# A decoder layer on one core: gate mask written first and rows added onto it by DMA, pooling means on ScalarE, two loads later, 187 pieces in another order

## The chip, the core and the metric

The program runs on one core of a Trainium2 chip. The core has a matrix engine (TensorE; its matmuls are "PE" in the profile and its weight loads "PEld"), three engines for elementwise work (VectorE "DVE", ScalarE "ACT", GpSimd "POOL"), and SyncE ("SP"), which here only issues transfers. Each engine takes its instructions strictly in the order of its own queue and waits on semaphores where it needs another engine's or a transfer's result. Transfers from SP's queue and from POOL's queue share 16 DMA engines.

The metric is the device time of one execution in microseconds, the median over runs. Lower is better.

## What is computed

One layer for 256 tokens of width 1024 in float32. The input `x` is normalised, multiplied with a wide matrix `w_in`, and the columns of the product feed three mixers side by side: a pooling mixer, a gated recurrent mixer with four heads (mLSTM) and causal attention with eight heads. Their outputs go through `w_out` and are added to `x`; then comes a gated feed-forward part with a short convolution.

```python
def pool_mixer(xp, w_pool, scale):          # four groups of 64 channels, windows 2, 4, 8, 16
    ...
        win_sum = cs[:, 1:, g] - cs[:, lo, g]
        outs.append(win_sum / cnt[None, :, None] - xg[:, :, g])   # cnt is smaller than w in the first tokens
    ...
def mlstm_chunkwise(q, k, v, i_pre, f_pre):
    ...
        logd = jnp.where(causal, g[..., :, None] - g[..., None, :] + ic[..., None, :], -jnp.inf)
        ...
        w = jnp.einsum('bhtd,bhsd->bhts', qc, kc) * jnp.exp(logd - mt[..., None])
...
        x = x + mix @ w_out[l]
        h2 = rmsnorm(x, ln2_g[l])
        u = causal_dwconv(h2 @ w_up[l], ffn_conv[l])
        x = x + (jax.nn.silu(u[..., :D_FF]) * u[..., D_FF:]) @ w_down[l]
```

## The kernel before

**Products.** To keep float32 accuracy on TensorE, each operand is split into a rounded part `hi` (ScalarE, line 214, rounded to the fp32r type) and the rest `lo` (VectorE, line 221, `raw - hi`). A product is then three matmuls: hi·hi, hi·lo and lo·hi. The weights come in "units" of 1 MB, loaded by SP into four rotating buffers `raw`, and each unit is split in two halves: pieces `("hi", u, q)` and `("lo", u, q)`. Units 0 to 10 are slices of `w_in`: 0 `of`, 1 `vi`, 2 `mq`, 3 `mk`, 4 and 5 the first attention heads (A), 6 `pool`, 7 and 8 the other heads (B), 9 and 10 the attention values (V). Then follow four units of `w_out`, eleven of `w_up` and eleven of `w_down`.

**The first microseconds.** `x` arrives transposed in eight slabs of 128 rows each together with the `of` columns (line 254), every slab a transfer of its own. VectorE scales each slab by the norm's gain (`first_full`, piece `("f", p)`, line 390, into `h_f`); TensorE multiplies it in plain float32 with the `of` weights (pieces `("of", t, p)`, line 511; the slab of `h_f` is the stationary operand, so its weight load waits for the `f` piece). The slabs are also squared in four quarters on ScalarE (`("sq", q)`, line 410; added up on VectorE, line 414), and split into `h_hi` (`("h", q)`, ScalarE, line 394) and `h_lo` (`("l", q)`, VectorE, line 398). The gain `g1` lies in the buffer of the first four slabs, so that buffer is free for unit 3 only when the last `f` piece has run.

**Order.** The mixer part of the program is a set of closures ("pieces"). Each has a place, a number from the table `PLACE` (line 44) or a default, and the pieces are emitted in the order of these numbers; an assertion keeps every piece behind those that it needs. The matmul groups stand at whole numbers from 4 on (`("b", n)`), so the table says between which matmul groups, and in which order on every engine, the small work is done. Nothing is rearranged later: a queue's order is the order of the places.

**Small work that the change touches.** The gates of the mLSTM go through a chain of scans on VectorE (pieces `pg`, `ga`, `gm`, `gs`, lines 640 to 660); the running maxima `mr` of the four heads are written to DRAM (`bm`, line 666), read back broadcast to all 128 partitions into `mb` (`br`, line 669), and GpSimd overwrites in the two diagonal blocks of each head what lies above the diagonal with 1e30 (`bs`, `affine_select`, line 674), so that `exp(a - mb)` gives zero there (`("wt", h)`, line 691). `("ct", name, j)` are the three taps of the short convolution on VectorE (line 539), `sig` the sigmoids on ScalarE between two table loads (lines 272, 548, 551), `("si", key)` the products that make the SiLU (line 555), `("mS", j)` the mLSTM's scores on TensorE (line 702), `("me", h)` their product with the decay (line 707), `("mN", t)` the product with the values (line 714). For attention, `("hq", ...)` and `("hs", ...)` are squares and their sums per head (lines 578, 584), `("kn", g)` the factors of the keys (lines 570 to 605), `("ke", g, t)` the scaled keys (line 610), `("kT", g)` and `("qT", g)` their transposes on TensorE (line 619), `("S", g, j)` the scores, `("PT", ...)` the transposed probabilities (line 816), `("pt", ...)` their copies (lines 822, 824) and `("O", g, j)` the products with the values (line 835).

**Pooling.** `pool_z` (lines 841 to 858) forms, for each half of the 256 channels, the window sums on GpSimd by doubling the width, copies the group with the smaller window along, multiplies with the table of 1/count (`rcnt`, 2 x 256 columns of `con`) and subtracts the channel itself, all in one piece. `pool_t` (line 862) multiplies the result with `pool_w`.

**Loads.** SP issues, in order: the eight slabs, unit 1 in two parts, unit 2, the parameters `par`, the constants `con` (512 KB, line 263), unit 3, the rows of `x` (`xs`, two transfers of 512 KB, line 403; first used by the residual after `w_out`), units 4 and so on. GpSimd's own queue carries, behind the pooling, the transfers `far` (line 1220) that prepare sums of `w_down` weights for the last stage.

Of the kernel before, what the change touches and what calls it, by code (L numbers as in the profile page):

```python
# [117 lines left out]
U_UP = U_OUT + N_OUT  # L118
U_DOWN = U_UP + NPAIR
N_UNITS = U_DOWN + N_DOWN  # L120


C_RCNT = 0
C_MN = C_RCNT + 2 * S
C_PW = C_MN + 256
C_END = C_PW + 2 * P


Q_G2 = 0
# [1392 lines left out]
```

## Time and profile before

| | |
|---|---|
| median of 3 runs | 295.83 us (295.75 to 296.02) |
| the profiled execution's own time | 295.97 us |
| its span, first to last instruction | 294.2 us |
| PE busy | 289.5 us, 98% |
| DVE / ACT / POOL busy | 260.1 / 209.3 / 44.7 us |
| TensorE clock granted | 1.00 throughout |

The span is 1.8 us shorter than the execution's time. In the views, a row of the timeline has a start, a duration, the engine, the line, the operation, `out<-in`, the shapes and how many instructions it stands for; in brackets is the engine's idle time ahead of it and what ended that. Instructions of one engine overlap in their pipelines: the time from one start to the next, not the duration, is what an instruction costs in its queue. A plain float32 matmul is two passes and shows as two.

### The profile page before, as it was taken

Reading aid. Unit: us, or ns where it says so; the run is one execution under the profiler, and the core shown is the slowest. Engines: PE = TensorE matmul, PEld = TensorE weight load, DVE = VectorE, ACT = ScalarE, POOL = GpSimd, SP = SyncE. Lnnn points to the kernel's source line nnn. Section 1 sums busy time; section 2 is a strip of 40 time slices with the busy share of each in tenths; the row PEclk is TensorE's granted clock in tenths of the full one; section 3 lists DMA queues with packets and bytes.
Section 4 is the critical chain, followed back from the end, with each engine's and each line's share of the span. In section 5 each row is a group of like instructions: output and inputs, shape, how many; then the busy total and the mean of one; then the engine's idle time right before and its main releaser. Section 6 shows DMA issues by size and latency. Waiting matters only on the chain.

```text
span 294.2 us, 4565 instructions
## 1 busy us (share of the span) xinstructions
PE 289.5 (98%) x1606; PEld 245.6 (83%) x1606; DVE 260.1 (88%) x518; ACT 209.3 (71%) x395; POOL 44.7 (15%) x73
## 2 busy tenths in 40 slices
PE   8999999999999999999999999999999999999995
PEld 4899888788778778888888888888988988888884
DVE  1978998999977757769999999999999989999992
ACT  3777779679895736987787787687677478786700
POOL 1000104724100005105015105105102110000000
PEclk9999999999999999999999999999999999999999
DMA  7999974079876576999998999997988988998003
GB/s 225 406 419 373 331 276 167 2 177 320 189 280 238 192 286 241 192 320 341 282 353 203 317 337 211 348 303 195 333 270 185 280 226 273 331 342 341 3 1 143
DMA packets 16599, 75.39 MB, mean 256 GB/s; under 512 B 1844, under 2 KB 2240, under 8 KB 10688
## 3 DMA queue, kind: packets, MB, share of 16 engines
q1 hardware_dynamic: 10384, 60.29, 54.3%
q0 software_dynamic: 6048, 14.68, 25.0%
q8 instruction: 12, 0.20, 0.3%
q10 hardware_dynamic: 144, 0.13, 0.1%
q14 instruction: 11, 0.09, 0.1%
HBM read 74.04 MB, written 15.73 MB: 305 GB/s over the span
## 4 chain that ended last, share of the span: by engine, by line
PE 87%; DVE 6%; ACT 3%; issue 2%; DMA 1%
PE up L1170 25%; PE up L1173 13%; PE wo L885 8%; PE dn L885 6%; PE m L1294 6%; PE dn L1294 5%; PE of L511 3%; DVE lo L221 2%; PE V L497 1%; PE V L499 1%; PE V L498 1%; PE upr L1103 1%; PE upr L1102 1%; PE upr L1101 1%; PE B L497 1%
## 5 line engine op out<-in xcount | busy, mean ns | idle before, releaser
L221 DVE TENSOR_TENSOR lo<-raw,hi 128x1024 fp32r<-128x1024 f32 (+2 forms) x74 | 83.7, 1148 | 4.6 <-ACT hi L214 4.6
L1170 PE MATMUL up<-h,hi 128*128 128x512 f32 x320 | 76.3, 391 | 0.0
L214 ACT ACTIVATE hi<-raw 128x1024 fp32r<-128x1024 f32 (+2 forms) x74 | 70.9, 983 | 6.2 <-DMA raw<-in_w 4.0
L1170 PEld LDWEIGHTS up<-h,hi 128*128 128x128 f32 x320 | 58.9, 188 | 11.4
L1173 PEld LDWEIGHTS up<-h,lo 128*128 128x128 f32 x320 | 41.0, 191 | 1.5
L1173 PE MATMUL up<-h,lo 128*128 128x256 f32 x320 | 41.6, 283 | 0.0
L1191 DVE SCALAR_TENSOR_TENSOR fy<-z,par,fy 128x255 f32<-128x255 f32 (+1 forms) x80 | 33.3, 479 | 0.0
L1220 POOL DMA_DIRECT2D far<-far x14 | 11.8, 840 | 106.6 <-DMA far<-in_w 55.4
L1220 POOL DMA_DIRECT2D far<-in_w x28 | 22.7, 1246 | 7.2 <-DMA far<-in_w 7.2
L1187 ACT ACTIVATE fy<-z,par 128x256 f32<-128x256 f32 x40 | 18.1, 502 | 1.7 <-DVE z L1180 1.2
L1201 ACT ACTIVATE fy<-fy 128x256 f32<-128x256 f32 x20 | 8.4, 418 | 12.2 <-DVE fy L1191 12.2
L1180 DVE TENSOR_TENSOR z<-up,zl 128x512 f32<-128x512 f32 x20 | 13.8, 688 | 3.0 <-ACT zl L1178 2.9
L1178 ACT ACTIVATE zl<-up 128x512 f32<-128x512 f32 x20 | 11.9, 594 | 4.0 <-PE up L1173 4.0
L221 DVE TENSOR_TENSOR lo<-more_raw,hi 128x1024 fp32r<-128x1024 f32 x12 | 14.6, 1218 | 0.0
L1294 PE MATMUL m<-ph,h 128*128 128x512 f32 x42 | 14.1, 389 | 0.0
L214 ACT ACTIVATE hi<-more_raw 128x1024 fp32r<-128x1024 f32 x12 | 12.6, 1053 | 0.0
L1208 ACT ACTIVATE a_hi<-a_sv 128x256 fp32r<-128x256 f32 (+1 forms) x16 | 5.7, 369 | 8.4 <-DVE a_sv L1203 8.4
L885 PE MATMUL wo<-hi,mix_hi 128*128 128x512 f32 x32 | 11.2, 411 | 0.0
L1329 ACT ACTIVATE ph<-sum 128x1024 fp32r<-128x1024 f32 x8 | 8.4, 1055 | 3.1 <-PE dn L1294 2.3
L885 PE MATMUL wo<-lo,mix_hi 128*128 128x512 f32 x32 | 10.6, 392 | 0.0
L885 PE MATMUL wo<-hi,mix_lo 128*128 128x512 f32 x32 | 10.6, 392 | 0.0
L1330 DVE TENSOR_TENSOR pl<-sum,ph 128x1024 fp32r<-128x1024 f32 x8 | 9.7, 1217 | 0.0
(331 smaller groups left out, 642.7 us busy)
## 6 DMA issues: line engine op xcount, KB each, us to landing
raw<-in_w SPq DMA_DIRECT2D x33, 1024.0 KB, 8.8
far<-in_w POOLq DMA_DIRECT2D x14, 512.0 KB, 11.1
more_raw<-in_w SPq DMA_DIRECT2D x6, 1024.0 KB, 8.6
sum<-far SPq DMA_DIRECT2D x4, 1024.0 KB, 6.8
far<-in_w POOLq DMA_DIRECT2D x14, 256.0 KB, 12.7
far<-far POOLq DMA_DIRECT2D x14, 256.0 KB, 7.4
more_raw<-far SPq DMA_DIRECT2D x3, 1024.0 KB, 8.2
raw<-in_w SPq DMA_DIRECT2D x4, 768.0 KB, 5.5
```

Of the source, the lines that this page charges most:

```text
L214: nc.scalar.activation(hi_t[u][:, s], raw_t[u][:, s], AF.Copy)
L221: nc.vector.tensor_sub(lo_t[u][:, s], raw_t[u][:, s], hi_t[u][:, s].bitcast(F32))
L885: nc.tensor.matmul(acc[t, c][:, :n], a, b[:, k, o:o + n], start=st and i == 0, stop=sp and i == 2)
L1170: nc.tensor.matmul(up_t[i][:, j], a, h_2[:, k].rearrange("p c t -> p (c t)"), start=k == 0, stop=False)
L1173: nc.tensor.matmul(up_t[i][:, j, :S], a, h_hi[:, k, :], start=False, stop=k == KT - 1)
L1178: nc.scalar.activation(zl, ps[:, :, S:], AF.Copy)
L1180: nc.vector.tensor_add(z, ps[:, :, :S], zl)
L1187: nc.scalar.activation(y_t[i, j], up_t[i][j], AF.Copy, scale=pcol(Q_FC + i + NPAIR * j + 4 * NPAIR))
L1191: nc.vector.scalar_tensor_tensor(y[:, d:], up_t[i][j][:, :S - d], pcol(Q_FC + i + NPAIR * j + 2 * NPAIR * tap), y[:, d:], op0=ALU.mult, op ...
L1220: nc.gpsimd.dma_start(s_far[i][:, at, :], src[:, block:block + 1, :].to_broadcast([P, at.stop - at.start, 512]), **({"accum_op": ALU.add} ...
L1294: nc.tensor.matmul(dst, a[x], b[y], start=start and n == 0, stop=stop and n == 2)
L1330: nc.vector.tensor_sub(l[:, s], src, h[:, s].bitcast(F32))
```

## The change

1. **Mask first.** GpSimd writes the mask into `mb` at the start of the program (1e30 above the diagonal, 0 elsewhere, from a constant). `spread_back` then adds the two diagonal blocks of the maxima onto it with an accumulating transfer from GpSimd's queue (512 KB), and SP loads only the third block (256 KB). The piece `bs` is gone; `br` now needs `setup`, and the decays wait for `br`.
2. **Pooling.** The window sums use two tiles in turn per half; the copies of the smaller group are gone. The first 16 tokens of each group are corrected by a small product on GpSimd (64 x 16), and the means are four ScalarE operations (64 x 256, a new piece `("pla", j)`) that multiply by 1/window. GpSimd subtracts the channel behind them. The 1/count table shrinks from 512 to 32 columns, so that `con` is 273 KB.
3. **Loads.** `con` is issued behind unit 6 and `xs` behind unit 11.
4. **Order.** 187 entries of `PLACE` differ. Two rows of the table, before and now:

```diff
-    ("f", 0): 1.75, ("of", 0, 0): 1.754813, ("f", 1): 1.7552, ("f", 2): 1.758, ("f", 3): 1.760807, ("of", 1, 0):
+    ("f", 0): 1.750626, ("of", 0, 0): 1.750984, ("sq", 0): 1.75217, ("f", 1): 1.753604, ("f", 3): 1.760807,
...
+    def load_rest(u):
+        if u == 6:
+            nc.sync.dma_start(con, consts)
+        if u == 11:
+            for t in range(NT):
+                nc.sync.dma_start(xs[:, t], x[t * P:(t + 1) * P])
...
+    mb = mpool.tile([P, 3, 4, P], F32, name="mb")
     nc.gpsimd.memset(ones, 1.0)
+    later_keys = mb.rearrange("p b h c -> p (b h) c")[:, :8, :]
+    nc.gpsimd.affine_select(later_keys, nc.const_aps.tensor_like(0.0, later_keys), [[0, 8], [1, P]], ALU.is_ge, -NEG,
+                            base=0, channel_multiplier=-1)
...
     def spread_back():
-        nc.sync.dma_start(mb, sb["far"].partition_broadcast(P))
-
-    def mask_max():
-
-        d = mb.rearrange("p b h c -> p (b h) c")[:, :8, :]
-        nc.gpsimd.affine_select(d, d, [[0, 8], [1, P]], ALU.is_ge, -NEG, base=0, channel_multiplier=-1)
+        nc.gpsimd.dma_start(mb[:, :2], sb["far"][:2].partition_broadcast(P), accum_op=ALU.add)
+        nc.sync.dma_start(mb[:, 2:], sb["far"][2:].partition_broadcast(P))
...
     def pool_z(j):
-        z = mid(f"plz{j}", 16 + S)
-        nc.gpsimd.memset(z[:, :16], 0.0)
+        z, *two = [mpool.tile([P, 16 + S], F32, name=f"pl{n}{j}") for n in "zab"]
+        for tile_ in (z, *two):
+            nc.gpsimd.memset(tile_[:, :16], 0.0)
         nc.vector.tensor_mul(z[:, 16:], ps_t["pool", j], rb)
...
-        d = mid(f"pld{j}")
-        nc.gpsimd.tensor_mul(d, cur[:, 16:], rcnt[:, j, :])
-        nc.gpsimd.tensor_sub(d, d, z[:, 16:])
+        sums, width = [z], 1
+        for n in range(2 + 2 * j):
+            r = slice(64 * (n == 1 + 2 * j), P)
+            cur = sums[-1]
+            sums.append(two[n % 2])
+            nc.gpsimd.tensor_add(two[n % 2][r, 16:], cur[r, 16:], cur[r, 16 - width:16 + S - width])
+            width *= 2
+        sb["plz", j], sb["pls", j] = z, sums[-2:]
+        for h in range(2):
+            r = slice(64 * h, 64 * h + 64)
+            few = sums[h - 2][r, 16:32]
+            nc.gpsimd.tensor_mul(few, few, con[r, C_RCNT + 16 * j:C_RCNT + 16 * j + 16])
+
+    def pool_mean(j):
+        d = sb["pls", j][1][:, 16:]
+        for h in range(2):
+            r = slice(64 * h, 64 * h + 64)
+            nc.scalar.activation(d[r, :], sb["pls", j][h][r, 16:], AF.Copy, scale=con[r, C_INV + j:C_INV + j + 1])
+        nc.gpsimd.tensor_sub(d, d, sb["plz", j][:, 16:])
         sb["pld", j] = d
```

**Place 1: ACT and DVE while the slabs arrive.** `sq` are the squares and their sums, `h<-h_f` the quarters of `h_hi` (ACT) and `h_lo` (DVE), `h_f<-head` the scaled slabs, `hi<-raw` the split of unit 1. ACT before:

```order
L410 ACTIVATE sq_112<-head_84 128x512
L394 ACTIVATE h_101<-h_f 128x2x256 x2
L410 ACTIVATE sq_112<-head_85 128x512
L410 ACTIVATE sq_112<-head_84 128x512
L394 ACTIVATE h_101<-h_f 128x2x256
L410 ACTIVATE sq_112<-head_85 128x512
```

and now, behind it the same stretch of DVE, before and now:

```order
L422 ACTIVATE sq_115<-head_88 128x512 x2
L408 ACTIVATE h_104<-h_f 128x2x256 x2
L422 ACTIVATE sq_115<-head_89 128x512 x2
L408 ACTIVATE h_104<-h_f 128x2x256
L226 ACTIVATE hi_163<-raw_90 128x520 x3
```

```order
L390 TENSOR_SCALAR h_f<-head_85,head_84 128x256
L398 TENSOR_TENSOR h_101<-h_f,h_101 128x2x256 x2
L390 TENSOR_SCALAR h_f<-head_85,head_84 128x256 x2
L414 TENSOR_TENSOR sq_112<-sq_112 128x512
L398 TENSOR_TENSOR h_101<-h_f,h_101 128x2x256
L390 TENSOR_SCALAR h_f<-head_85,head_84 128x256
```

```order
L404 TENSOR_SCALAR h_f<-head_89,head_88 128x256
L412 TENSOR_TENSOR h_104<-h_f,h_104 128x2x256
L404 TENSOR_SCALAR h_f<-head_89,head_88 128x256 x2
L426 TENSOR_TENSOR sq_115<-sq_115 128x512
L412 TENSOR_TENSOR h_104<-h_f,h_104 128x2x256 x2
L404 TENSOR_SCALAR h_f<-head_89,head_88 128x256
```

On ACT the second square (slabs 2 and 3) stands ahead of the first two quarters of `h_hi`, and the fourth ahead of the third quarter. On DVE the `h_lo` operation that is first in its row is now that of the second quarter, which needs ACT's second quarter; the first quarter's stands, with the third's, ahead of the last slab.

**Place 2: DVE around the SiLU products**, from the last taps on (`mqT`, `mkT` with their head pair's number, `sg` the sigmoids, `gm` the output gate, `lo6`, `lo7` splits of units 6 and 7, `plz0` the first pooling half, `akAss` sums of the keys' squares). Before:

```order
L555 TENSOR_TENSOR mkT0_489<-mkT0_489,sg_510 128x256
L555 TENSOR_TENSOR mqT0_432<-mqT0_432,sg_508 128x256
L555 TENSOR_TENSOR mkT1_491<-mkT1_491,sg_514 128x256
L555 TENSOR_TENSOR mqT1_436<-mqT1_436,sg_512 128x256
L221 TENSOR_TENSOR lo7_519<-raw7_352,hi7_475 128x1024
L558 TENSOR_TENSOR gm_122<-gm_122,con_81 128x256 x2
```

and now:

```order
L566 TENSOR_TENSOR mqT0_436<-mqT0_436,sg_508 128x256
L569 TENSOR_TENSOR gm_124<-gm_124,con_81 128x256
L566 TENSOR_TENSOR mkT1_491<-mkT1_491,sg_514 128x256
L233 TENSOR_TENSOR lo6_463<-raw6_265,hi6_395 128x1024
L595 TENSOR_REDUCE akAss_531<-akAsq0_524 128x4
L233 TENSOR_TENSOR lo7_533<-raw7_354,hi7_478 128x1024
L566 TENSOR_TENSOR mkT0_488<-mkT0_488,sg_510 128x256
L233 TENSOR_TENSOR lo7_533<-raw7_354,hi7_478 128x1024
L569 TENSOR_TENSOR gm_124<-gm_124,con_81 128x256
L566 TENSOR_TENSOR mqT1_447<-mqT1_447,sg_512 128x256
```

The four products stood together; now three splits, two gate products and a sum stand between the first and the last of them. Both halves of unit 6 stood ahead of the products, and one of them stands among them now.

**Place 3: PE at the transposes of the keys.** `akAT` is the transposed keys of the first heads, `B0` their successors' product with unit 7. Before:

```order
L354 MATMUL pool1_630<-h_2_101,lo6_465 128x256
L497 MATMUL B0_682<-hi7_475,h_2_101 128x512
...
L499 MATMUL B0_682<-hi7_475,h_2_101 128x512
L619 MATMUL akAT_689<-ident_78,knA0_628 128x128
L619 MATMUL akAT_689<-ident_78,knA1_643 128x128
```

and now:

```order
L368 MATMUL pool1_625<-h_2_104,lo6_463 128x256
L630 MATMUL akAT_670<-ident_78,knA0_623 128x128
L630 MATMUL akAT_670<-ident_78,knA1_638 128x128
L630 MATMUL akAT_670<-ident_78,knA0_623 128x128
L630 MATMUL akAT_670<-ident_78,knA1_638 128x128
L508 MATMUL B0_678<-hi7_478,h_2_104 128x512
```

The four transposes have moved ahead of the six matmuls of `B0`.

More of the change, by code (lines that the diff above doesn't have):

```diff
@@ L44 @@
 PLACE = {
[41 rows of a table removed]
-    0): 37.567146, ("hi", 10, 1): 37.567846, ("plh", 1): 37.667, ("pll", 1): 37.833, ("hs", "aqB", 1): 38.333,
[20 rows of a table removed]
[25 rows of a table added]
+    "aqA", 0): 25.281211, ("qe", "aqA", 0): 25.323988, ("hs", "akA", 1): 25.374871, ("hm", "akA"): 25.400403,
[39 rows of a table added]
 }
@@ L123 @@
 C_RCNT = 0
-C_MN = C_RCNT + 2 * S
+C_INV = C_RCNT + 2 * 16
+C_MN = C_INV + 2
 C_PW = C_MN + 256
@@ L204, in load @@
         nc.sync.dma_start(raw[:, :n], src)
+        load_rest(u)
     def load_next(u, x=0):
@@ L262 @@
     nc.sync.dma_start(par, params)
-    nc.sync.dma_start(con, consts)
-    rcnt = con[:, :C_MN].rearrange("p (j c) -> p j c", c=S)
     g2 = par[:, Q_G2:Q_G2 + KT]
@@ L401, in next_loads @@
         load(RAW_BUFS - 1)
-        for t in range(NT):
-            nc.sync.dma_start(xs[:, t], x[t * P:(t + 1) * P])
         load(RAW_BUFS)
@@ L459 @@
     mask = mpool.tile([P, S], F32, name="mask")
-    mb = mpool.tile([P, 3, 4, P], F32, name="mb")
     gg = mpool.tile([P, 1], F32, name="gg")
@@ L472, in setup @@
         nc.gpsimd.memset(v_aug[:, :, :, 64:65], 1.0)
-        nc.gpsimd.memset(mask, 0.0)
-        nc.gpsimd.affine_select(mask, mask, [[-1, S]], ALU.is_ge, NEG, base=P, channel_multiplier=1)
+        nc.gpsimd.affine_select(mask, nc.const_aps.tensor_like(0.0, mask), [[-1, S]], ALU.is_ge, NEG, base=P,
+                                channel_multiplier=1)
     def setup_gain():
@@ L841, in pool_z @@
     def pool_z(j):
-        z = mid(f"plz{j}", 16 + S)
-        nc.gpsimd.memset(z[:, :16], 0.0)
+        z, *two = [mpool.tile([P, 16 + S], F32, name=f"pl{n}{j}") for n in "zab"]
+        for tile_ in (z, *two):
+            nc.gpsimd.memset(tile_[:, :16], 0.0)
         nc.vector.tensor_mul(z[:, 16:], ps_t["pool", j], rb)
-        low, high = WIN[2 * j], WIN[2 * j + 1]
-        cur, width = z, 1
-        while width < high:
-            nxt = mid(f"plz{j}{width}", 16 + S)
-            nc.gpsimd.memset(nxt[:, :16], 0.0)
-            r = slice(0, P) if 2 * width <= low else slice(64, P)
-            nc.gpsimd.tensor_add(nxt[r, 16:], cur[r, 16:], cur[r, 16 - width:16 + S - width])
-            if 2 * width > low:
-                nc.gpsimd.tensor_copy(nxt[:64, 16:], cur[:64, 16:])
-            cur, width = nxt, 2 * width
-        d = mid(f"pld{j}")
-        nc.gpsimd.tensor_mul(d, cur[:, 16:], rcnt[:, j, :])
-        nc.gpsimd.tensor_sub(d, d, z[:, 16:])
+        sums, width = [z], 1
[16 more added lines that the diff above has]
+        nc.gpsimd.tensor_sub(d, d, sb["plz", j][:, 16:])
         sb["pld", j] = d
@@ L971 @@
     put("bm", spread_max, "gs")
-    put("br", spread_back, "bm")
-    put("bs", mask_max, "br")
+    put("br", spread_back, "bm", "setup")
     put("gc", gate_cols_t, "gs")
@@ L978 @@
         put(("plz", j), do(pool_z, j), "rb", "setup", done["pool", j])
-        put(("ply", j), do(pool_t, j), ("plz", j), at=(27.9, 23.9)[j])
+        put(("pla", j), do(pool_mean, j), ("plz", j))
+        put(("ply", j), do(pool_t, j), ("pla", j), at=(27.9, 23.9)[j])
         put(("plh", j), do(pool_hi, j), ("ply", j))
@@ L992 @@
     for h in range(4):
-        put(("wt", h), do(decay, h), "bs", "gco")
+        put(("wt", h), do(decay, h), "br", "gco")
     for j in range(2):
@@ L1492, in _consts @@
     c = np.zeros((P, C_END), np.float32)
-    t = np.arange(S) + 1.0
+    t = np.arange(16) + 1.0
     for g in range(4):
-        b = C_RCNT + S * (g // 2)
+        b = C_RCNT + 16 * (g // 2)
         r = slice(64 * (g % 2), 64 * (g % 2) + 64)
-        c[r, b:b + S] = 1.0 / np.minimum(t, WIN[g])
+        c[r, b:b + 16] = WIN[g] / np.minimum(t, WIN[g])
+        c[r, C_INV + g // 2] = 1.0 / WIN[g]
         b = C_PW + P * (g // 2) + 64 * (g % 2)
```

123 rows, old and new, of the table PLACE are left out of this document.

## The prediction
> **What bounds the kernel now.** I read the windows by stage first, then what PE's weight loads wait for.
>
> ```profile
> 0.00:12.00 12.00, 11.03 (x40) 7.09 (x41) 5.92 (x14) 6.38 (x10) 1.39 (x9) 1.00 0.84 295
> 12.00:112.00 100.00, 99.80 (x613) 83.95 (x612) 86.63 (x214) 75.78 (x174) 16.17 (x30) 1.00 0.72 250
> 112.00:288.00 176.00, 176.00 (x936) 152.12 (x935) 166.20 (x291) 127.17 (x213) 27.16 (x34) 1.00 0.86 262
> ```
>
> The numbers behind a window's length are the busy times of PE, PEld, DVE, ACT and POOL, then PE's clock. PE sets the end in every stage: behind 12 us it is busy for 275.8 of 276, at clock 1.00, while the others have 10% and more to spare. From the list of waits, those of PE's weight loads in the stages that the change touches:
>
> ```profile
> PEld of L511 <- DVE h_f L390: 1.8, 3, 1.0
> PEld akAT L619 <- issue: 0.5, 1, 0.5
> PEld mq L354 <- DVE lo L221: 0.2, 1, 0.2
> ```
>
> The diff removes no matmul from PE and adds none, so it can only take such waits away or make new ones. These three total 2.5 us, and 1.8 of it is the slabs' arrival, which no order hastens. So a gain of more than 1 us has nothing to come from. A loss has no such limit: behind 12 us PE has no slack in which a delay could be caught up.
>
> **The change part by part.** All times below are places in the profiled execution.
>
> *(a) The start.* The timeline of ACT, of DVE and of PE:
>
> ```profile
> 4.35 0.63 ACT L410 ACTIVATE sq<-head 128x512 f32<-128x512 f32 x1 [2.26 <-DMA head<-in_xt]
> 4.89 0.61 ACT L394 ACTIVATE h<-h_f 128x512 fp32r<-128x512 f32 x1
> ```
>
> ```profile
> 6.57 0.35 DVE L390 TENSOR_SCALAR h_f<-head 128x256 f32<-128x256 f32 x1 [0.37 <-DMA head<-in_xt]
> ...
> 7.58 1.29 DVE L398 TENSOR_TENSOR h<-h_f,h 128x512 fp32r<-128x512 f32 x2
> ...
> 10.51 0.35 DVE L390 TENSOR_SCALAR h_f<-head,head 128x256 f32<-128x256 f32 x1
> ```
>
> ```profile
> 11.73 0.47 PE L362 MATMUL vi<-hi,h 128*128 128x260 f32 x1
> ```
>
> Before, ACT used its wait for slab 3 (whose `f` runs on DVE at 6.57, when the slab has landed) for the first quarter of `h_hi`. Now the second square, which reads that slab, stands ahead of the first two quarters. It starts at 6.6; at ACT's spacing of 4.89 − 4.35 = 0.54 the quarters start at 7.15 and 7.7, and the second ends, 0.61 later, at 8.3. The first `l` in DVE's row is now the one that needs this second quarter, so it starts at 8.33, not at 7.58. Behind it, up to the last slab's `f`, stand the same operations as before (three `l`, two `f`, one sum of squares): 10.51 − 7.58 = 2.93. The last `f` runs at 11.26. PE's last `of` matmuls need it, and `vi` starts 11.73 − 10.51 = 1.22 behind it: at 12.48, 0.75 later than before. PE may get through some of the earlier slabs' work in the added wait, so some of the 1.22 can shrink. Bounds: 0, if the slabs land late enough that DVE waits for the last one anyway; 0.9, if DVE is held by something more. I take +0.65, near the upper end, because each of these rows is the direct predecessor of the next.
>
> *(b) The transposes.* PE's timeline:
>
> ```profile
> 46.68 0.39 PE L352 MATMUL pool<-h,hi 128*128 128x256 f32 x1
> ...
> 49.65 0.40 PE L497 MATMUL B<-hi,h 128*128 128x512 f32 x1
> ...
> 50.81 0.39 PE L499 MATMUL B<-hi,h 128*128 128x512 f32 x1
> 51.34 0.79 PE L619 MATMUL akAT<-ident,knA 128*128 128x128 f32 x4
> 51.97 0.60 PE L619 MATMUL aqAT<-ident,aqA 128*128 128x128 f32 x4
> 52.41 1.00 PE L714 MATMUL num<-v_aug,mb 128*128 128x65 f32 x8
> ```
>
> From `akAT` to `aqAT` it took 0.63; from `aqAT` to `num`, four transposes too, 0.44. From 50.81 to `akAT` it took 0.53, where a matmul of `B` needs (50.81 − 49.65) / 5 = 0.23. So 0.5 us were a wait for the keys. Now PE meets `akAT` six matmuls, 1.4 us, sooner. Either the keys come that much earlier, or a new wait takes the place of this one.
>
> *(c) DVE ahead of the transposes.* The group of DVE's splits from 25.7 to 41.6 us, then DVE's timeline, POOL's and ACT's:
>
> ```profile
> L221 DVE TENSOR_TENSOR lo<-raw,hi 128x1024 fp32r<-128x1024 f32 x7 | 9.3, 1337 | 0.0
> ```
>
> ```profile
> 25.72 1.21 DVE L221 TENSOR_TENSOR lo<-raw,hi 128x1024 fp32r<-128x1024 f32 x1
> ...
> 34.99 2.11 DVE L221 TENSOR_TENSOR lo<-raw,hi 128x1024 fp32r<-128x1024 f32 x1
> ...
> 41.68 1.22 DVE L221 TENSOR_TENSOR lo<-raw,hi 128x1024 fp32r<-128x1024 f32 x1
> 42.82 0.42 DVE L555 TENSOR_TENSOR mkT<-mkT,sg 128x256 f32<-128x256 f32 x1
> 43.15 0.42 DVE L555 TENSOR_TENSOR mqT<-mqT,sg 128x256 f32<-128x256 f32 x1
> ```
>
> ```profile
> 34.86 1.17 POOL L674 TENSOR_SCALAR_AFFINE_SELECT mb<-mb 128x1024 f32<-128x1024 f32 x1 [32.71 <-DMA mb<-far]
> 49.23 0.75 POOL L857 TENSOR_TENSOR pld<-pld,plz 128x256 f32<-128x256 f32 x1
> ```
>
> ```profile
> 42.73 1.28 ACT L272 ACT_TABLE_LOAD   x1
> 44.99 0.46 ACT L578 ACTIVATE akAsq<-A,n1r 128x256 f32<-128x256 f32 x1
> 45.35 0.50 ACT L691 ACTIVATE mb<-mb,cols 128x256 f32<-128x256 f32 x1
> ```
>
> The stretch from 25.72, behind the gates, to the end of the taps at 41.68 is 15.96 long. The gates come from PE, so its begin shifts by (a), taken at 0.7 at the most, to 26.42. Seven splits were in it, at 42.82 − 41.68 = 1.14 from start to start, but one took 2.11 while GpSimd wrote the mask. Now six are in it and no mask: −1.14 − 0.9 = −2.04. The taps end at 26.42 + 15.96 − 2.04 = 40.34, 1.34 sooner than before. The sigmoids on ACT follow, and ACT has its second table at 42.73 + 1.28 − 1.34 = 42.7.
>
> DVE's row behind the taps is now: product `mq0` and a gate product (0.33 each, 43.15 − 42.82), product `mk1` when ACT's last sigmoid is there (41.41), split 6, the sum `akAss` when ACT has squared its input (42.7 + 0.46 = 43.18), split 7 at 43.5, product `mk0` at 44.65, the other split 7 at 45.0, a gate product at 46.1, and last product `mq1`, from 46.45 to 46.87. PE reads it in the second half of `mS`:
>
> ```profile
> 45.18 1.58 PE L702 MATMUL mS<-mqT,mkT 64*128 64x256 f32 x16
> ```
>
> Half of the 1.5 up to 46.68 and the 0.7 of (a) bring PE there at 45.18 + 0.75 + 0.7 = 46.63; it waits until 46.92, +0.3. From there to `akAT` it has 0.75 and the last pool matmuls, 49.65 − 46.68 = 2.97: it meets `akAT` at 50.64. DVE meanwhile goes on to the keys; its rows before:
>
> ```profile
> 47.59 0.42 DVE L584 TENSOR_REDUCE akAss<-akAsq 128x4 f32<-128x256 f32 x1 [0.88 <-ACT akAsq L578]
> ...
> 48.27 1.01 DVE L707 SCALAR_TENSOR_TENSOR mb<-mS,mb 128x384 f32<-128x384 f32 x2
> 49.34 0.66 DVE L570 SCALAR_TENSOR_TENSOR aknt<-akr 128x8 f32<-128x8 f32 x1
> ...
> 50.77 0.76 DVE L610 TENSOR_TENSOR knA<-A,akr 128x256 f32<-128x256 f32 x2
> ```
>
> The second `akAss` started at 47.59 and now starts at 47.1 (46.45 and two operations of 0.33). From it to `knA` it was 3.18, with two products with `mS` (1.01) of which one is left: 47.1 + 3.18 − 0.5 = 49.8, and both `knA` are there at 50.55. GpSimd's additions of the pooling fall into this stretch, and may add 0.3: at 49.34 a tiny operation of 128x8 took 0.66, up to the end of GpSimd's at 49.98. So `akAT` starts between 50.65 and 50.85, takes 0.44, `B0` 1.4, and `aqAT` starts at 52.5 to 52.7 instead of 51.97. (a), (b) and (c) together: +0.5 to +0.7. Of the +0.65 and +0.3, only about 0.35 comes back from the 0.5 of (b).
>
> The Trainium skill ("SBUF — State Buffer", section "Who interferes with whom") says that a VectorE instruction with two SBUF inputs and a GpSimd instruction that reads SBUF exclude each other for the whole instruction. The 2.11 beside the mask agrees. By the rule the pooling's additions hold the key factors in the change too, which gives the upper end, +0.7; without it, +0.5.
>
> *(d) Covered edits.* The adding transfer starts when `far` has landed, about 28.5 + 0.7, and the decays read `mb` at 45.35 − 1.3, about 44. The nearest rows, of 512 KB from GpSimd's queue (by line 1220 half of them add too), and where `mb` was loaded:
>
> ```profile
> 28.50 0.33 SPq L669 DMA_DIRECT2D mb<-far  x1
> ...
> far<-in_w POOLq DMA_DIRECT2D x14, 512.0 KB, 11.1
> ```
>
> 29.2 + 11.1 = 40.3, so 3.7 us of cover: 0 (without it, one for one). The four pooling means are 45.35 − 44.99 = 0.36 each by ACT's row of that width, 1.44 in all, and stand ahead of this row, in whose wait they fit:
>
> ```profile
> 65.70 0.21 ACT L564 ACTIVATE hmnt<-hv 128x4 f32<-128x4 f32 x1 [1.55 <-DVE hv L739]
> ```
>
> So 0, and up to 1.4 for ACT's exponentials behind it if that cover were gone. `con` is now first read by the gate products at 40.8, and its issue lies some 15 us ahead of that; `xs` is read behind `w_out`, after 100: 0, with DVE waiting one for one otherwise. One group of `PT` transposes now stands directly ahead of the products `OB` that read its copy. Eight products of another group come first:
>
> ```profile
> 97.44 0.65 PE L835 MATMUL OB<-ptsB,av 128*64 128x256 f32 x4
> ...
> 98.14 0.60 PE L835 MATMUL OB<-ptsB,av 128*64 128x256 f32 x4
> ```
>
> They take 98.14 − 97.44 = 0.70, against a copy of about the size of DVE's half-wide product with `mS` above (0.5) and its start behind the transposes: 0 to 0.15, I take 0.05.
>
> **Sum.** (a) to (c) +0.6 and (d) +0.05: +0.65 on the profiled execution's 295.97 (span 294.2, with 1.8 around it) is 296.62. That execution lies 0.14 above the median of 295.83, so against the median I forecast 296.5.
>
> **Rivals.**
>
> *The other side (0.32): no slower.* (a) comes, but DVE keeps ahead of PE: `mq1` ends before 46.6 and the keys are there before 50.3. Then the 0.5 of (b) is saved for good, and +0.65 + 0.05 − 0.5 = +0.2 gives 296.0, no change. For it speak the 1.34 that the taps gain, and that DVE is late by 0.3 only in my working. Against it: three splits of 1.14 stand ahead of `mq1`, and ACT's table, not DVE, sets when `akAss` can start. It decides at `mq1`'s end, at 46.6.
>
> *The start costs nothing (0.10).* If DVE's row waits for the last slab anyway, (a) is 0 and (b) is saved: 295.83 − 0.5 = 295.3. Against it: the last `f` shows no wait before it.
>
> *The addition comes late (0.07).* If adding to a target takes twice the 11.1, `mb` is there at 51.4, 7.4 after it is wanted; the products with `mS` and `num` at 52.4 then move, and some 1.5 of it reaches PE through `num`: 298.0.
>
> *GpSimd's queue comes late (0.07).* The first weights for the last stage were fetched at 58.6, behind the pooling:
>
> ```profile
> L1220 POOL DMA_DIRECT2D far<-in_w x28: 579/1322/1513, 58.6 to 223.1; - x28
> ```
>
> The subtraction ahead of them now waits for ACT's means, which stand ahead of 65.70. They start 7 us later and meet the loads of the units between 70 and 90; a split that is held for 1 us there makes it 297.5.
>
> **How the numbers follow.** The forecast has 0.44: 296.5, with its own range of 296.2 to 296.9. The range for all cases is 295.5 to 297.3; it leaves out most of the second rival and of the third and half of the fourth, about 0.2. A measurement of this kernel can tell about 0.2% from no change, 0.59 us. Slower by more than that, above 296.42: 0.28 of the forecast, 0.14 of the two late cases and 0.04 of the first rival, 0.46. Within it: 0.16 of the forecast, 0.28 of the first rival and 0.02 of the second, 0.46. Faster: 0.08, the second rival's rest.
>
> **What would show it.** Right: the last `f` at 11.3 and `vi` at 12.4; no split of 2 us; ACT's second table ready at 42.7; `mq1` at 46.4 with a wait of 0.3 inside `mS`; `akAT` at 50.7, right behind `knA`; `aqAT` at 52.5 to 52.7, and every later stage shifted alike. Wrong: `vi` at 11.7; `akAT` at 50.4 or sooner; decays that wait for `mb`; or a stage behind 60 us that is longer than before.

## The result, and the profile after

The change made the kernel slower: 297.3 us, the median of 4 runs (297.15 to 297.59), against 295.92 (295.75 to 296.11) for the kernel before on the same chip. The ratio is 1.0052 [1.004, 1.0065]. The profiled execution took 297.15, its span is 295.4, which is 1.2 more than before in both.

The windows by stage of the changed kernel, with the columns that the prediction explains:

```profile
0.00:12.00 12.00, 10.53 (x37) 6.83 (x38) 5.47 (x13) 6.53 (x11) 2.15 (x9) 1.00 0.84 303
12.00:112.00 100.00, 99.29 (x611) 83.93 (x610) 84.02 (x210) 76.50 (x173) 13.54 (x27) 1.00 0.71 247
112.00:288.00 176.00, 176.00 (x935) 152.06 (x934) 167.17 (x294) 128.28 (x218) 27.65 (x35) 1.00 0.86 260
```

DVE is busy 2.6 us less between 12 and 112 us (84.02 against 86.63); part of that is work that now falls behind 112 us (210 instructions in this window against 214), and over the whole execution it is 258.4 us against 260.1. PE, which sets the end, is busy less too, and that is the loss: 0.5 us in each of the first two stages. What its weight loads wait for behind the slabs:

```profile
PEld akBT L630 <- ACT hi L226: 0.6, 1, 0.6
PEld pool L368 <- DVE lo L233: 0.5, 1, 0.5
PEld mS L709 <- DVE mqT L566: 0.4, 1, 0.4
```

The waits before `akAT` and `mq` are gone. Three others stand here, and the prediction named one of them, that before `mS`. (The releaser in these rows is inferred. `akBT` reads the scaled keys `knB`, and their rows below show that DVE ended that wait, not ACT.)

PE's timeline of both kernels, read side by side, shows where the 1.2 us arise. The times are the starts of the matmuls named, in the profiled executions.

| PE reaches | before | change | later by | what happened ahead of it |
|---|---|---|---|---|
| `vi`, first | 11.73 | 12.37 | 0.64 | the last `f` runs later |
| `A`, last | 41.99 | 42.41 | 0.42 | the waits of before ahead of `mq` and of the norm's row swallow 0.2 |
| `mS`, first | 45.18 | 46.19 | 1.01 | the third `pool` matmul waits 0.5 and starts again: +0.6 |
| `pool`, second half | 46.68 | 48.14 | 1.46 | the second half of `mS` waits: +0.44 |
| `aqAT` | 51.97 | 52.94 | 0.97 | the wait before `akAT` is gone: −0.5 |
| `num`, last | 59.59 | 60.38 | 0.79 | −0.2; from `aqAT` to here 7.44 instead of 7.62, as with the mask alone (`e8`, 7.42) |
| `akBT` | 73.90 | 75.05 | 1.15 | `akBT` waits: +0.36 |
| `OB`, last | 98.69 | 100.02 | 1.33 | +0.17 |
| `up`, first | 123.07 | 124.27 | 1.20 | a wait in the second norm is gone: −0.13 |
| last of the tail | 290.41 | 291.60 | 1.19 | nothing more |

The start, on ACT, then on DVE:

```profile
4.38 0.63 ACT L422 ACTIVATE sq<-head 128x512 f32<-128x512 f32 x1 [2.29 <-DMA head<-in_xt]
6.50 0.63 ACT L422 ACTIVATE sq<-head 128x512 f32<-128x512 f32 x1 [1.49 <-DMA head<-in_xt]
7.04 1.14 ACT L408 ACTIVATE h<-h_f 128x512 fp32r<-128x512 f32 x2
```

```profile
8.21 0.69 DVE L412 TENSOR_TENSOR h<-h_f,h 128x512 fp32r<-128x512 f32 x1 [0.76 <-ACT h L408]
...
11.18 0.35 DVE L404 TENSOR_SCALAR h_f<-head,head 128x256 f32<-128x256 f32 x1
```

ACT waits 1.49 for slab 3 and only then makes the quarters. DVE waits 0.76 for the second quarter. That is the chain of step (a).

DVE from the taps to the keys, then PE's answers, and behind them the third `pool` matmul of the kernel before:

```profile
37.48 0.42 DVE L537 TENSOR_TENSOR mkz<-mk,rb 128x256 f32<-128x256 f32 x1 [0.51 <-DVE mqT L550]
...
40.83 0.43 DVE L566 TENSOR_TENSOR mqT<-mqT,sg 128x256 f32<-128x256 f32 x1
...
42.10 1.22 DVE L233 TENSOR_TENSOR lo<-raw,hi 128x1024 fp32r<-128x1024 f32 x1
...
46.82 0.42 DVE L566 TENSOR_TENSOR mqT<-mqT,sg 128x256 f32<-128x256 f32 x1
...
47.93 0.43 DVE L600 TENSOR_SCALAR akAss<-akAss 128x8 f32<-128x8 f32 x1
...
50.23 0.75 DVE L621 TENSOR_TENSOR knA<-A,akr 128x256 f32<-128x256 f32 x2
```

```profile
42.75 0.28 PE L367 MATMUL pool<-h,hi 128*128 128x256 f32 x1
43.37 0.39 PE L368 MATMUL pool<-h,lo 128*128 128x256 f32 x1 [0.34 <-DVE lo L233]
...
47.29 0.92 PE L709 MATMUL mS<-mqT,mkT 64*128 64x256 f32 x8 [0.18 <-DVE mqT L566]
...
51.11 0.60 PE L630 MATMUL akAT<-ident,knA 128*128 128x128 f32 x4
52.94 0.60 PE L630 MATMUL aqAT<-ident,aqA 128*128 128x128 f32 x4
```

```profile
42.45 0.28 PE L354 MATMUL pool<-h,lo 128*128 128x256 f32 x1
```

The split at 42.10 is the first half of unit 6. PE's third `pool` matmul is its first reader. It would have run at 42.87 (its neighbours are 0.12 apart) and starts at 43.37; the next one follows 0.22 behind it, so that PE loses 0.6. `akAT` starts right behind the last `pool` matmul, at 51.11, with the keys in time. Also new here is a gap of 0.51 ahead of the second `mkz`, which waits for nothing that is late: the tap before it is DVE's own and had ended. The last experiments return to it.

The keys of the other heads, on DVE, and their transposes on PE:

```profile
74.10 0.48 DVE L883 SCALAR_TENSOR_TENSOR mix_lo<-ply,par,mix_hi 128x256 fp32r<-128x256 f32 x1
74.49 0.42 DVE L621 TENSOR_TENSOR knB<-B,akr 128x256 f32<-128x256 f32 x1
```

```profile
75.05 0.63 PE L630 MATMUL akBT<-ident,knB 128*128 128x128 f32 x4 [0.19 <-DVE knB L621]
```

and the keys in the kernel before:

```profile
72.96 0.74 DVE L610 TENSOR_TENSOR knB<-B,akr 128x256 f32<-128x256 f32 x2
```

The two halves of the keys ran one behind the other, and now `mix_lo`, a piece of the pooling's output, stands between them and takes 0.39 of the row (74.49 − 74.10). The second half is ready at 74.91, and PE starts 0.14 later.

### The profile page after: what moved, and what is told of

Its sections match the earlier page's. It is cut to its first block, busy times and chain, and to the rows that moved or that the text cites. A ratio compares the mean times of both kernels' runs of the same rounds, so it can differ in the third digit from the quotient of the medians.

```text
span 295.4 us, 4565 instructions
## 1 busy us (share of the span) xinstructions
PE 289.7 (98%) x1606; PEld 246.3 (83%) x1606; DVE 258.4 (87%) x518; ACT 211.3 (72%) x399; POOL 43.3 (15%) x71
## 4 chain that ended last, share of the span: by engine, by line
PE 82%; DVE 11%; ACT 2%; issue 1%; DMA 1%; SPq 0%; DVEq 0%
PE up L1184 25%; PE up L1187 13%; PE wo L899 8%; PE dn L899 6%; PE m L1308 6%; PE dn L1308 5%; DVE lo L233 4%; PE of L522 2%; DMA head<-in_xt 1%; PE upr L1116 1%; PE upr L1117 1%; PE upr L1115 1%; PE tail L899 1%; DVE mqT L550 1%; DVE prA L791 1%
## 5 line engine op out<-in xcount | busy, mean ns | idle before, releaser
L233 DVE TENSOR_TENSOR lo<-raw,hi 128x1024 fp32r<-128x1024 f32 (+2 forms) x74 | 82.3, 1131 | 1.9 <-ACT hi L226 1.9
L1192 ACT ACTIVATE zl<-up 128x512 f32<-128x512 f32 x20 | 11.9, 594 | 4.8 <-PE up L1187 4.8
```

Source lines behind the costliest of these rows:

```text
L233: nc.vector.tensor_sub(lo_t[u][:, s], raw_t[u][:, s], hi_t[u][:, s].bitcast(F32))
L1192: nc.scalar.activation(zl, ps[:, :, S:], AF.Copy)
```

## Experiments

Each kernel is the changed one with the edit shown, unless it says otherwise. `e1` to `e4` ran on one chip with the kernel before at 295.82, `e5` to `e8` on one with 295.71, `e9` and `e10` with 295.77, `e11` and `e12` with 295.67. Comparisons across these groups go by the ratio to the kernel before.

**`e1_start`: the start in the old order.**

```diff
-    ("f", 0): 1.750626, ("sq", 0): 1.75217, ("sq", 1): 2.125142, ("l", 0): 2.916246, ("f", 7): 2.956442, ...
+    ("f", 0): 1.75,     ("sq", 0): 2.25,    ("sq", 1): 2.7,      ("l", 0): 2.532718, ("f", 7): 3.064854, ...
```

29 places of the first slabs' pieces have their values of before.

> The change, with the places of the start pieces (f, of, sq, h, l and the splits of unit 1) put back to those before; nothing else. Theory A (each PE delay is passed on whole): the last f runs at 10.5, vi starts at 11.7 instead of 12.37, and everything behind shifts by the same 0.64, because the waits at the pool product and at mS hang on DVE work that itself starts from PE's gates: 296.7. Rival B (the waits near 43 and 47 us are set by something that does not start from PE, such as the raw loads): they grow by what the start gives back, and the time stays at 297.2 to 297.3.

Measured: 296.37 (10 runs), ratio 1.0022 [1.0012, 1.0031], so 0.9 us came back. `vi` started at 11.92. The waits before `mS` (0.34) and `akBT` (0.36) remained, but what PE loses at `pool` shrank from 0.6 to 0.2 (the fourth matmul starts at 42.72, and would have at 42.54), though no piece around it was moved. This was more than the start alone explains. DVE's second `mkz`, in this kernel's timeline, has a gap of only 0.11 ahead, too short for the view to show:

```profile
36.62 0.42 DVE L537 TENSOR_TENSOR mkz<-mk,rb 128x256 f32<-128x256 f32 x1
```

**`e7_before_start`: the other way round,** the kernel before with those 29 places of the change.

> The kernel before, with only the start's places of the change (f, of, sq, h, l and the splits of unit 1). Theory A: vi starts at 12.4 to 12.8 instead of 11.7, and all of the 0.65 to 0.9 reaches the end, 296.5 to 296.7 against 295.85. Rival B (other parts of the change are needed for it, such as the mask that GpSimd now writes in the same microseconds): vi at 11.7 to 11.9 and 295.9.

Measured: 296.33 (10 runs), ratio 1.0021 [1.0012, 1.003]. So the order of the start costs about 0.6 us by itself. `vi` started at 12.56, 0.83 later than in the profile of before; of that, 0.2 was swallowed before the last `A` (half of it by the wait before `mq`), and another 0.2 at `akAT`, whose wait of 0.5 shrank. In this pair of traces 0.37 of it reaches the last matmul; the 0.6 is from the medians. Over all traces, `vi` started at 11.5 to 11.9 with the old order (five kernels, mean 11.72) and at 12.3 to 12.8 with the new one (nine kernels, mean 12.57). The difference is 0.85, and the execution profiled first lay at its low end with 0.64.

**`e2_split6`: the first half of split 6 ahead of the last six taps,** in time for the third `pool` matmul.

```diff
-    ("lo", 6, 0): 22.557874
+    ("lo", 6, 0): 20.9898
```

> The change, with one DVE operation moved: the first half of split 6 stands ahead of the last six taps again, instead of between the SiLU products. Rival B (the waits at the pool product, 0.6, and at mS, 0.45, are separate costs): the first goes, 296.7. Theory A (both are one DVE row that is too long before the products): the wait of 0.6 at the third pool matmul goes, but the taps end 1.14 later, the sums of the keys' squares wait for ACT's table, mk0 ends at about 46.0 and mq1 at about 47.9, and PE waits that much more inside mS: second half of mS at 47.9 against 47.29, 297.9.

Measured: 298.18, ratio 1.0079 [1.0064, 1.0094], 0.8 slower than the change. The wait before `pool` went, and both halves of `mS` waited instead (the list of PE's weight loads' waits):

```profile
PEld mS L709 <- DVE mqT L566: 1.1, 1, 1.1
PEld mS L709 <- DVE mkT L566: 0.7, 1, 0.7
```

A split of 1.14 moved ahead of the taps pushes everything behind them. DVE's row sets PE's time in this stretch, and taking one wait away there is not the same as shortening the row.

**`e3_products`: the same, and the four products together** ahead of both halves of split 7.

```diff
-    ("lo", 6, 0): 22.557874, ("si", ("mk", 0)): 23.040533,  ("si", ("mq", 1)): 25.059724
+    ("lo", 6, 0): 20.9898,   ("si", ("mk", 0)): 22.5577665, ("si", ("mq", 1)): 22.557767
```

> As the run before (first half of split 6 ahead of the last taps), and the four SiLU products together again, ahead of both halves of split 7. Theory A: both halves of mS start without a wait (45.6 and 46.3), so PE is 1.04 earlier at the transposes of the keys, 50.1; but the key factors still come behind split 7, a gate product and the second sum, at about 51.0, so a wait of 0.9 appears there and the time is 297.1. Rival B (the waits at the pool product and mS are all that stands between): 296.3.

Measured: 297.31, ratio 1.0052 [1.0037, 1.0067], just the change's time. `mS` waited no more, and the next reader of DVE's row took the wait over:

```profile
PEld akAT L630 <- PE pool L368: 0.9, 1, 0.9
```

```profile
50.76 0.74 DVE L621 TENSOR_TENSOR knA<-A,akr 128x256 f32<-128x256 f32 x2
```

(Again the releaser's name is wrong: `knA` runs until 51.50, when PE has long done its `pool` matmuls.) The three waits at `pool`, `mS` and `akAT` are thus one lag of DVE, met at different places.

**`e4_means`: ACT's pooling means behind the second square for the mLSTM's norm.**

```diff
-    ("pla", 1): 33.093373, ("pla", 0): 33.182671
+    ("pla", 1): 33.2991,   ("pla", 0): 33.2992
```

In the change, the list of ACT's and DVE's operations shows the means ahead of that square, and DVE waiting for it:

```profile
63.75 0.50 ACT L870 ACTIVATE plb<-pla,con 64x256 f32<-64x256 f32 x1
...
65.33 0.51 ACT L870 ACTIVATE plb<-plb,con 64x256 f32<-64x256 f32 x1
65.86 0.42 ACT L740 ACTIVATE hsq<-hm 128x256 f32<-128x256 f32 x1
```

```profile
66.31 0.42 DVE L745 TENSOR_REDUCE hv<-hsq 128x4 f32<-128x256 f32 x1 [0.49 <-ACT hsq L740]
```

> The change, with ACT's four pooling means moved behind the second square of the mLSTM's rows instead of between the two (one ACT instruction changes places with four). Theory A (the means, 0.52 each, make the second square 2.1 late; DVE idles 0.5 at its sum and has the keys of the second heads 0.4 late, so that PE waits at their transposes): PE's wait of 0.36 before akBT goes, and the time falls by 0.35 to 296.95. Rival B (DVE's row before these keys is longer for its own order, with the division and one product of the mixer's output moved ahead): the wait stays, 297.3.

Measured: 297.35, ratio 1.0052 [1.0037, 1.0067]: nothing gained, and `akBT` waited 0.36 as before. The theory that the means' place makes this wait fell. What DVE gained by the earlier square it lost again: its two operations on `hv`, which took 0.26 and 0.17 in the change, now ran beside GpSimd's subtractions (DVE's timeline of `e4`, then GpSimd's):

```profile
65.96 0.36 DVE L746 TENSOR_SCALAR hv<-hv 128x4 f32<-128x4 f32 x1
...
66.68 0.70 DVE L746 TENSOR_SCALAR hv<-hv 128x4 f32<-128x4 f32 x1
```

```profile
65.56 0.73 POOL L871 TENSOR_TENSOR plb<-plb,plz 128x256 f32<-128x256 f32 x1 [9.89 <-ACT plb L870]
66.62 0.74 POOL L871 TENSOR_TENSOR plb<-plb,plz 128x256 f32<-128x256 f32 x1 [0.32 <-ACT plb L870]
```

**`e6_keys_b`: two pieces on DVE earlier,** a scaling of probabilities (`("dv", "A", 1)`) and the first half of the keys `knB`.

```diff
-    ("dv", "A", 1): 35.183339, ("ke", "B", 0): 38.056727
+    ("dv", "A", 1): 33.7333,   ("ke", "B", 0): 37.51
```

> The change, with two DVE places moved at the second heads: the division of the first probabilities between the two row sums (where DVE idled 0.5), and the key product of the first rows ahead of the mixer's output, directly behind the other key product. Rival B of the run before last, now the theory (DVE's own order makes the second heads' keys late, not the means on ACT): the wait of 0.36 before akBT goes and the time falls to 296.95. Against it: if the means on ACT set it after all, DVE idles elsewhere and the wait stays, 297.3.

Measured: 296.9, ratio 1.0041 [1.0027, 1.0054]. `akBT` started at 74.59 without the wait of 0.36, as expected: from the first `vi` to `akBT` PE takes 62.31, in the change 62.68. The medians' ratios differ by as much, but their intervals overlap. The keys in DVE's timeline:

```profile
73.65 0.74 DVE L621 TENSOR_TENSOR knB<-B,akr 128x256 f32<-128x256 f32 x2
```

They run one behind the other again. The first half starts 0.12 sooner than in the change, the second is done at 74.39, 0.52 sooner, which is the 0.39 of `mix_lo` more. The scaling that was moved along brought the first half no further than that 0.12. With the means at the change's place, the wait is gone: it was the piece between the halves.

**`e8_before_mask`: the kernel before with part 1 alone,** the mask written first and the maxima added onto it.

```diff
+    mb = mpool.tile([P, 3, 4, P], F32, name="mb")      # at the start of the program, with the affine_select of 0 and 1e30
...
-        nc.sync.dma_start(mb, sb["far"].partition_broadcast(P))
+        nc.gpsimd.dma_start(mb[:, :2], sb["far"][:2].partition_broadcast(P), accum_op=ALU.add)
+        nc.sync.dma_start(mb[:, 2:], sb["far"][2:].partition_broadcast(P))
...
-        put(("wt", h), do(decay, h), "bs", "gco")
+        put(("wt", h), do(decay, h), "br", "gco")
```

> The kernel before, with only the mask written first and the rows added onto it by a transfer from GpSimd's queue. Theory A (the mask held a split of DVE for 0.9, and DVE's row leads to the keys): no split of 2 us, the SiLU products and the keys 0.9 earlier, the 0.5 of wait at akAT gone, 295.35. Rival B (the row to the keys waits for ACT's table and not for DVE, or the transfer is late): akAT at 51.3 as before and 295.85.

Measured: 295.17 (295.09 to 295.54, 11 runs), ratio 0.9985 [0.9976, 0.9994], the lowest ratio of all, though the interval of `e5` below overlaps it. Its timelines of DVE and of PE:

```profile
34.83 1.22 DVE L221 TENSOR_TENSOR lo<-raw,hi 128x1024 fp32r<-128x1024 f32 x1
...
49.74 0.76 DVE L613 TENSOR_TENSOR knA<-A,akr 128x256 f32<-128x256 f32 x2
```

```profile
50.65 0.40 PE L502 MATMUL B<-hi,h 128*128 128x512 f32 x1
50.89 0.60 PE L622 MATMUL akAT<-ident,knA 128*128 128x128 f32 x4
```

The split that took 2.11 takes 1.22, the keys come 1.03 sooner than before, and `akAT` follows the matmul ahead of it with no wait: the 0.5 that step (b) found is saved, in the old order.

**`e9_parts_1_to_3`: the change's code with the table of before,** and the means (new pieces) at 33.34 and 33.35.

> The change's mask, pooling and loads, with every place of the table as before; ACT's four pooling means stand behind the second square of the mLSTM's rows. Theory A (the loss lies in the reordering alone; the mask's 0.5 stays, and the second norm's transposes may gain some 0.2, because in the change PE did not wait for them): 295.0 to 295.2. Rival B (the means on ACT and GpSimd's later subtractions cost PE a wait at the second heads' keys or at their transposes, about 0.4): 295.5. Rival C (the loads of the constants and of x at their new times hold a weight unit): 296 or more, with a split that waits for a transfer.

Measured: 295.57 (294.92 to 296.25, 12 runs), ratio 0.9996 [0.9986, 1.0006], so not told from before, and some 0.3 above `e8` by the ratios, with intervals that overlap. `akAT` doesn't wait here either. A wait is longer at 97.6 us, where ACT needs a unit of weights; the rows are ACT's waits in `e9`, in `e8`, and the transfers `far` in `e9`:

```profile
ACT hi L226 <- DMA raw<-in_w: 2.3, 1, 2.3
```

```profile
ACT hi L214 <- DMA raw<-in_w: 0.5, 1, 0.5
```

```profile
L1234 POOL DMA_DIRECT2D far<-in_w x28: 572/1336/1502, 64.8 to 223.1; - x28
```

The transfers for the last stage start 6.2 us later than before (64.8 against 58.6), behind GpSimd's subtraction, which waits for ACT's means. PE waited 0.3 at 101.8 for `mix_lo`, which stands on DVE behind the two splits of that unit. ACT waited 2.1 for a unit at 86.5 too, where before it waited 0.5. That they took the transfer engines from the unit's load fits these rows; it was not tried apart.

**`e10_ptb`: the transposes `PT` of the second heads in the order of before** (14 places, of `PT`, `pt`, `dv`, `da`, `O`, `oh` of `B`).

> The change, with the transposes of the second heads' probabilities in one row of twelve again, as before. A look at the trace: from the end of the scores SB to the last OB the change takes 14.56, before it was 14.39. Theory A (each of the three added switches between a matmul of 512 columns and transposes costs PE some 0.09): 14.3. Rival B (a switch costs nothing): 14.56.

Measured in one run: 297.41. From the end of the scores `SB` to the last `OB` it took 14.53, in the change 14.56, before 14.39. So the order of these pieces costs nothing. In `e9`, with the old order and the new code, it was 14.54, in `e8` 14.40. It is no wait that makes the 0.15 or so: in this stretch stand 42 matmuls of `wo`, each of 512 columns, and in the timelines they start some 230 ns apart in the kernel before, `e7` and `e8`, and 232 to 234 ns apart in the change and in every run with its pooling and loads. The granted clock is 1.00 in both. What in that code slows them is open.

**`e11_one_more` and `e12_two_more`: one, and two, more instructions on DVE at the start,** of which nothing depends. The gap of 0.51 ahead of the second `mkz` showed in the change, `e2`, `e3` and `e4`, `e6` and `e10` (0.505 to 0.525 each), where this `mkz` is the 64th record of DVE's queue, waits that have a record of their own counted. In `e1` and `e5` it is the 65th, and the gap is 0.11 and 0.10. To move the count without moving any work:

```diff
+    spare = mpool.tile([P, 2], F32, name="spare")
+    nc.vector.memset(spare[:, 0:1], 0.0)
+    nc.vector.memset(spare[:, 1:2], 0.0)    # e12 only
```

> The change with one instruction more on DVE: a memset of one column of a tile that nobody reads, at the very start, where DVE is idle until 4.6 us. In every trace of the change's own mixer order with the change's start, DVE stood still for 0.5 before the second mkz, 0.5 behind its own last operation, and mkz was the 64th record of its queue; with the start of before it was the 65th, and the gap was 0.1. Theory F (it is the place in DVE's instruction stream that costs the 0.5): mkz becomes the 65th, the gap falls to 0.1, split 6 is 0.4 earlier, PE's wait of 0.5 at the third pool matmul goes, and with the rest of DVE's row 0.4 earlier the time is 296.85. Theory G (it is the timing of the start): gap and wait stay, 297.3.

> The same with two such memsets: mkz is the 66th record. Theory F: no gap of 0.5 there, and none at the instruction that is now the 64th, if the cost belongs to a wait at that place; a gap at another instruction, if it belongs to the place alone. Theory G: the gap of 0.5 ahead of mkz stays.

Measured: `e11` 296.91 (9 runs), ratio 1.0041 [1.0027, 1.0054]; `e12`, one run, 296.78. In `e11` this row, the split of unit 6 and the third `pool` matmul read

```profile
37.16 0.42 DVE L537 TENSOR_TENSOR mkz<-mk,rb 128x256 f32<-128x256 f32 x1
...
41.77 1.22 DVE L233 TENSOR_TENSOR lo<-raw,hi 128x1024 fp32r<-128x1024 f32 x1
```

```profile
43.05 0.39 PE L368 MATMUL pool<-h,lo 128*128 128x256 f32 x1
```

with 0.11 of idle time ahead of `mkz`. PE lost 0.2 at `pool` and no longer 0.6 (the fourth matmul starts at 43.27, and would have at 43.08), and `mS` started at 45.88, although `vi` started at 12.47. From the first `vi` to the last matmul PE took 278.75, in the change 279.23. The ratio is lower by 0.3 us, which by itself isn't told from the change's, as the intervals overlap. In `e12` the gap was 0.10 and the same stretch 278.73. The new tile may also have moved other tiles in memory; that was not tried apart, but `e1` and `e5` have the short gap without it.

**`e5_combined`: all mendings of the order at once.** The start as in `e1`, split 6 and products as in `e3`, the second heads as in `e6`, and around the first keys:

```diff
-    ("gg", 0): 22.557737, ("gg", 1): 25.046142, ("hs", "akA", 1): 25.374871, ("hm", "akA"): 25.400403
+    ("gg", 0): 28.645,    ("gg", 1): 28.924,    ("hs", "akA", 1): 23.5,      ("hm", "akA"): 23.51
-    ("hg", "akA"): 25.471403, ("ke", "A", 0): 25.929, ("ke", "A", 1): 26.439728
+    ("hg", "akA"): 25.1,      ("ke", "A", 0): 25.865, ("ke", "A", 1): 25.87
```

> The change, with the start of before, the first half of split 6 ahead of the last taps, the four SiLU products together, and DVE's way to the keys of the first heads shortened: the second sum of squares behind the first half of split 7, both gate products behind the keys, the two key products ahead of the products with mS; and at the second heads the division of the first probabilities between the two row sums and both key products together. Theory A (every wait of PE that the change brought is one of DVE's order, and all of them can go): no wait at the pool product, in mS, at akAT or at akBT; PE ends 0.9 earlier than before, 295.0 to 295.3 against 295.85. Rival B (taking one wait away brings the next, as the run that moved split 6 alone did): at least 0.5 of it comes back, no faster than 295.7.

Measured: 295.35 (11 runs), ratio 0.9988 [0.9979, 0.9997]. It is faster than both kernels, than the one before by a little, and no faster than `e8`. The only waits left in this stretch:

```profile
PEld akAT L630 <- DVE mb L714: 0.2, 1, 0.2
...
PEld akBT L630 <- issue: 0.2, 1, 0.2
```

With 41 places put otherwise, 29 of them as before, the changed kernel is 0.36 us faster than before and no longer 1.4 slower. So its code is not what made it slow.

## Why the prediction was right and wrong

The direction was right, and 297.3 lies at the edge of the range. The size was wrong: 1.4 more than before where +0.65 was forecast. One reading at the start was too generous, though nothing in the sum rests on it: between 112 and 288 us DVE has 5.6% to spare (166.20 of 176), not 10%. By its steps:

**(a) The start: right in its chain, and near in size.** Square, quarter, first `l` and last `f` ran at 6.50, 7.04, 8.21 and 11.18, forecast at 6.6, 7.15, 8.33 and 11.26; `vi` at 12.37, forecast 12.4. Over all traces the shift is 0.85, not 0.65, and by `e7` it is worth 0.6 at the end. The sentence that PE has "no slack in which a delay could be caught up" behind 12 us was too strict: the 0.2 that PE waited before `mq`, a row that the prediction itself quotes, is such slack, and so is the 0.5 before `akAT`.

**(b) The transposes: right.** The wait of 0.5 is gone. But `e8` shows that it needed no order: the mask's removal alone ends it.

**(c) DVE ahead of the transposes: the step that failed.** The forecast ran DVE's row as "product `mk1` when ACT's last sigmoid is there (41.41), split 6, ...", and gave a wait to the last product alone. That one was right: 0.3 forecast, 0.34 measured, 0.44 with PE's start again. What was left out is the reader of that split. PE's third `pool` matmul needs the first half of unit 6. By the forecast's own row that split began at 41.74 (41.41 and a product of 0.33) and ended, 1.22 later, at 42.96; PE was at this matmul at 42.45 before, and with the forecast's shift of 0.7 it came there at 43.15. The two were never set side by side, and so a margin of 0.2 passed as no question at all. Both sides of it were off. PE came at 42.87, since its shift was 0.42 there. The first product ran at 40.83, not at 40.34, mostly through the gap of 0.51 before the second `mkz`, so that the split ended at 43.32. That made the 0.6, which the sum had at nothing. `e11` separates the two: without the gap the split starts at 41.77, as forecast, and PE still loses 0.2, because it comes sooner than forecast. There the rest of the step comes out too: PE is at the second half of `mS` at 46.63 (45.88 + 0.75; forecast 46.63), its operand starts at 46.50 (forecast 46.45), and `aqAT` at 52.63, inside the forecast of 52.5 to 52.7; in the change it started at 52.94. So 0.3 of what the sum lacked is the gap, which no row of the kernel before showed. The bound of 0.3 for GpSimd's additions was about right in size: the operation on `akAss` of 128x8 took 0.43 beside an addition, and 0.17 in `e8`, where one ran beside it for the first 0.08 only; the three key factors, for which it was meant, took 0.17 each. The Trainium skill ("SBUF — State Buffer", section "Who interferes with whom") says that a VectorE `tensor_scalar` that runs in a two-port mode and a GpSimd instruction exclude each other until the one that was first has ended. The rows of `e4` agree: the 0.36 and the 0.70 end at 66.32 and 67.38, just behind GpSimd's 66.29 and 67.36.

**(d) The covered edits: three of four.** The addition took 11.3, about the 11.1 of the row that the forecast used, though all of `mb` (768 KB) had come in 6.3 by SP's queue before. It was issued at 27.8 and landed in time: the decays read `mb` at 43.41 with no wait. So the rival "the addition comes late" is out:

```profile
mb<-far POOLq DMA_DIRECT2D x1, 512.0 KB, 11.3
```

No engine's list of waits names `con` or `xs`, as forecast.

The means were taken at 0.36 each and took 0.52, 2.1 in all and not 1.44, and were not covered: DVE waited 0.49 behind them. By `e4` and `e6`, though, that is not what PE met. The first half of `knB` starts 0.81 later than before, no more than PE itself is late by then (0.79 at `num`); the second is later by another 0.39, the `mix_lo` between them, and that is the wait of 0.36 before `akBT`. The prediction looked at the places around the first keys only and took "every later stage shifted alike". This failed, and it is the second term that was missing, 0.36. The third, 0.17 between the scores and `OB`, was forecast there at 0.05; by `e10` the order, the reason given, is not its cause. It is in the slower matmuls of `wo`, which come with the change's code and not with its order.

**The rivals.** "No slower" did not come about with this order, but its mechanism, the 0.5 of (b) saved for good, is what `e8` shows, and in `e9` `akAT` doesn't wait either. "The start costs nothing" is refuted by `e7`. "GpSimd's queue comes late" was right about the transfers, which started at 66.6 in the change, 8 us later than before; but there no split between 70 and 90 us waited for a unit. In `e9` ACT did wait for units, 2.1 at 86.5 and 2.3 at 97.6, and PE waited 0.3 behind the second; that the late transfers are the reason is not shown.

## What to carry to other kernels

Where a piece is moved back in a busy engine's row, look up the first reader of every piece in that row and set its time beside the new end, also where the sum leaves it a margin: the margin of 0.2 at split 6 was used up when PE came 0.2 sooner than forecast (`e11`), and the gap of 0.51 came on top (the change). An engine's lag shows as several waits of the bottleneck, one behind the other; mending one moves it on to the next (`e2`, `e3`), and only a shorter row removes it. And a change that bundles code with an order is best run with the old order first: here all of the code with the old order was level with the kernel before (`e9`), its first part alone 0.15% faster (`e8`), and with the new order it was 0.5% slower.

## What was not expected of the hardware

An idle time of 0.51 us on VectorE appeared ahead of the second `mkz`, which stands behind a wait, in all six traces of the change's code in which it was the 64th record of its queue. It was 0.10 or 0.11 in the four traces in which one or two records more stood ahead of it with the taps in the same order; in `e11` and `e12` these were dead memsets of one column each. In `e7` the second `mkz` is the 64th too, stands directly behind a split, and has no gap; in `e11` the 64th record is the wait ahead of `mkz` and in `e12` a tap, and neither is followed by a gap of that size. So the place alone isn't enough, and what else it takes is not known. Its mechanism stays open: no run shows what the engine did in that time.

The matmuls of `wo`, with the same shapes, operands and granted clock, start some 230 ns apart with the old pooling and loads and 232 to 234 ns with the new. Nothing waits between them; the reason is open.

The start scatters by 0.5 us from trace to trace (`vi` between 12.28 and 12.78 with one and the same order), which is as much as most terms of the sum above. A single profile can't settle a step of this size; the medians of ten runs can.
